# One tile for state and u, the centring of v in a matmul, and the substitution's blocks stored straight from the masked scores

## The chip, the cores and the metric

The kernel runs on one core of one Trainium2 chip. TensorE (PE), VectorE (DVE), ScalarE (ACT) and GpSimd (POOL) compute; SyncE (SP) issues every DMA of this kernel, in order, and 16 DMA engines move the data. The metric is the time of one execution on the device in microseconds (us), the median of three runs.

## The reference

The program is a decoder trunk of two layers on a sequence of 1024 positions with 1024 channels, in float32. Layer 1 is an RWKV-7 mixer: projections r, k, v and a gate g of token-shifted inputs, two small low-rank paths for decay and a, and then a recurrence per head (16 heads of 64), cut to what matters here:

```python
kk = kk / max(sqrt(sum(kk * kk)), 1e-12)            # per head
state = state * w_t + sa * b_t + v_t * k_t           # sa = state . a_t, a = -kk, b = kk * ah
y_t = state . r_t
yn = (y - mean(y)) * rsqrt(var(y) + eps)             # per head, so v may be centred beforehand
```

The normalized y, a bonus and silu(g) go through an output matrix. Layer 2 is differential attention on keys and values from layer 1's output. Both layers end in a residual sum.

## The kernel before

Layer 1 begins with norms, low-rank paths and the first projections (about 0 to 260 us). Then the recurrence runs in chunks of 64 positions. A tile is 2 chunks of 8 heads (4 pairs); 16 tiles go one after another, software-pipelined over slots: in slot i, `chain` works on tile i, `norm` on tile i-1, `merge` on tile i+1, `invert` on tile i+2 and `prep` on tile i+3. Between their instructions stand those of the remaining projections and of the output projection (`proj_step`, `out_proj`), which give PE most of its work. Layer 2 follows from about 900 us on.

The order on each engine is not written out by hand: every instruction is recorded, and a planner that simulates the engines, with priorities for chain, merge, invert and prep, sets the order in which each engine, SP too, meets its instructions. Engines then work strictly in that order.

The parts that the change touches:

- `proj_step`, projection of v (p == 2): the 128x512 result `ev` is transposed in four pieces on PE (L211), DVE sums each head's 64 values (L215), subtracts the mean while it copies to SBUF (L217), and SP stores the centred v to DRAM, `d_vc` (L220). Tiles `ev` come from a pool `evp` with two buffers, which the output projection also uses (loads of x, stores of x2).
- `prep`: the masked scores `pm` hold, for each chunk, the triangular blocks (32 by 32) that a forward substitution has to invert. The squared norms of k come from a matmul with the matrix `last`, which puts them in row 31 of each block and zeros elsewhere; ACT copies them into `ab` (L485), DVE adds the masked scores (L510), and one DMA stores `ab` to DRAM as `dA` (L511). L528 reads `dA` back as `al`, 4 copies for 4 groups of partitions.
- `invert`: DVE divides by the norms (L538 to L540), POOL substitutes row by row (L551, L553), SP stores `xx` as `dX` (L556) and loads it in another layout as `qd` (L558), which `merge` needs (L576 on DVE).
- `merge` and `chain`: `uv` holds v and, later, u; `sv` holds v again (copied by ACT, L608) and the state. The chain is z (L639), a copy (L642), u (L649), copies into `uv` (L651, L652), the state's update (L658, L661, L665, L666), and the output y from two groups of matmuls (L629 from the state, L632 from u and v).

```python
        nc.sync.dma_start(out=dA.rearrange("c x s t -> (x s) c t"), in_=ab)          # L511
        nc.sync.dma_start(out=dX.rearrange("x k q t -> q x k t"), in_=xx)            # L556
        nc.sync.dma_start(out=al, in_=dA.rearrange("c x s t -> (c x) (s t)").unsqueeze(0).to_broadcast([4, 32, 1024])) # L528
```

SP meets a DMA, waits for the semaphores that it needs, and issues it; whatever stands behind it waits too.

Of the kernel before, what the change touches and what calls it, by code (L numbers as in the profile page):

```python
# [20 lines left out]
P = 128  # L21
# [3 lines left out]
C = 64  # L25
# [51 lines left out]
class Trunk:  # L77
# [10 lines left out]
    def start(self, lp, xnT):  # L88

        nc, tc, I = self.nc, self.tc, self.I  # L90
        const = self.const
        self.ident = const.tile([P, P], F32, name="ident")
        make_identity(nc, self.ident)
        self.par = const.tile([P, len(ROWS), KT], F32, name="par")
# [14 lines left out]
        for t0 in range(0, KT, 2):  # L109
            ms = lp.tile([P, 2], F32, name="ms")  # L110
            for i in range(2):
                sq = lp.tile([P, D], F32, name="sq", bufs=1)
# [3 lines left out]
            for i in range(2):  # L116
# [5 lines left out]
                for hf in range(2):  # L122
                    pt = self.fps.tile([P, 4, P], F32, name="fl")
# [36 lines left out]
    def proj_step(self, hf, p, pr, src, group):  # L160

        nc, I = self.nc, self.I
        sl = slice(hf * TH, (hf + 1) * TH)
        G = {"w": []}
# [31 lines left out]
        def post(k):  # L196
            if k == 0:
                G["ev"] = ev = self.evp.tile([P, TH], F32, name="ev")
                if p == 3:
                    nc.scalar.activation(ev, G["ps"], AF.Sigmoid)  # L200
                    nc.vector.tensor_tensor(ev, ev, G["ps"], op=ALU.mult)
                else:
                    nc.scalar.copy(out=ev, in_=G["ps"])
                nc.sync.dma_start(out=self.d_in[p][pr, :, sl], in_=ev)
            if p != 2:
                return

            if k == 2:
                G["pt"] = pt = self.fps.tile([P, 4, P], F32, name="fl")
                for i in range(4):  # L210
                    nc.tensor.transpose(out=pt[:, i, :], in_=G["ev"][:, i * P:(i + 1) * P], identity=self.ident)  # L211
            if k == 4:
                ptv = G["pt"].rearrange("p i (h e) -> p (i h) e", e=64)
                mn = self.evp.tile([P, 8], F32, name="mn")
                nc.vector.tensor_reduce(mn, ptv, axis=AX.X, op=ALU.add)  # L215
                vc = self.evp.tile([P, 4, P], F32, name="ev")
                nc.vector.scalar_tensor_tensor(vc.rearrange("p i (h e) -> p (i h) e", e=64),  # L217
                                               mn.unsqueeze(2).to_broadcast([P, 8, 64]), -1.0 / 64, ptv,
                                               op0=ALU.mult, op1=ALU.add)
                nc.sync.dma_start(out=self.d_vc[sl, pr * P:(pr + 1) * P].rearrange("(i p) e -> p i e", p=P), in_=vc)  # L220
# [174 lines left out]
    def wkv_open(self):  # L395
        nc, tc = self.nc, self.tc
# [26 lines left out]

        self.last = cst.tile([P, P], F32, name="last")
        nc.gpsimd.memset(self.last, 0.0)
        for o in (0, 64):
            nc.gpsimd.memset(self.last[o:o + 64, o + 31:o + 64:32], 1.0)
# [15 lines left out]
    def prep(self, M, following):  # L443
# [31 lines left out]
        nc.tensor.matmul(nps.rearrange("p c t -> p (c t)"), lhsT=self.last, rhs=sq.rearrange("p u t -> p (u t)"), start=True, stop=True)  # L475
# [56 lines left out]
    def invert(self, M):  # L532
# [24 lines left out]
        M["qd"] = qd = self.ub.tile([P, 8, 32], F32, name="qd", bufs=1)  # L557
        nc.sync.dma_start(out=qd, in_=dX.rearrange("(c x) k q t -> (x k q) c t", c=8))  # L558

    def merge(self, M):  # L560
# [6 lines left out]
        M["sv"] = sv = self.ub.tile([P, 2, 8, C], F32, name="sv")  # L567
# [39 lines left out]
        for h in range(2):  # L607
            nc.scalar.copy(out=sv[64 - h * 64:P - h * 64, h], in_=uv[64 - h * 64:P - h * 64, h])  # L608

    def chain(self, M):  # L610

        nc, sm, ps = self.nc, self.sm, self.wps
        ar, pm, uv, sv, bkt, q, wc = (M[n] for n in ("ar", "pm", "uv", "sv", "bkt", "q", "wc"))
        HS = [slice(h * 64, h * 64 + 64) for h in range(2)]
        wt = self.state[M["j"]]
        for h in range(2):
            nc.scalar.copy(out=sv[HS[h], h, 0::NC, :], in_=wt[HS[h]])
        yield 1

        def out(c):  # L620
            if c == 0:
                M["y"] = ps.tile([P, 8, C], F32, name="y", bufs=1)
            y = M["y"]

            z = M["qt"] + c == 0
            pairs = [(u * NC + c, h) for u in range(NU) for h in range(2)]

            for uc, h in [] if z else pairs:
                nc.tensor.matmul(y[HS[h], uc, :], lhsT=sv[HS[h], h, uc, :], rhs=ar[HS[h], uc, 1, :], start=uc == c, stop=False,  # L629
                                 tile_position=(h * 64, h * 64))  # L630
            for uc, h in pairs:
                nc.tensor.matmul(y[HS[h], uc, :], lhsT=uv[:, h, uc, :], rhs=pm[:, h, uc, 64:P], start=z and uc == c,  # L632
                                 stop=uc == pairs[-1][0], tile_position=(0, h * 64))
        for c in range(NC):
            us = [(u, u * NC + c) for u in range(NU)]
            zp = ps.tile([P, NU, C], F32, name="zu", bufs=2)
            for u, uc in us:
                for h in range(2):
                    nc.tensor.matmul(zp[HS[h], u, :], lhsT=pm[:, h, uc, 0:64], rhs=sv[:, h, uc, :], start=True, stop=True,  # L639
                                     tile_position=(0, h * 64))  # L640
            zs = sm.tile([P, NU, C], F32, name="zs", bufs=1)
            nc.scalar.copy(out=zs, in_=zp)  # L642
            if c:
                out(c - 1)
# [9 lines left out]
            if M["qt"] < S // TM - 1 or c < NC - 1:  # L654
                sp = ps.tile([P, NU, C], F32, name="zu", bufs=2)
                for u, uc in us:
                    for h in range(2):
                        nc.tensor.matmul(sp[HS[h], u, :], lhsT=bkt[:, h, uc, :], rhs=uv[:, h, uc, :], start=True, stop=True,  # L658
                                         tile_position=(0, h * 64))
                tn = sm.tile([P, NU, C], F32, name="tn", bufs=1)  # L660
                nc.vector.tensor_tensor(tn, wt, sp, op=ALU.add)  # L661
                wb = wc[:, c::NC].unsqueeze(2).to_broadcast([P, NU, C])
                if c < NC - 1:
                    for h in range(2):
                        nc.vector.tensor_tensor(sv[HS[h], h, c + 1::NC, :], tn[HS[h]], wb[HS[h]], op=ALU.mult)  # L665
                nc.gpsimd.tensor_tensor(wt, tn, wb, op=ALU.mult)  # L666
            yield 1
        out(NC - 1)

    def norm(self, M):  # L670
# [3 lines left out]
        y = nm.tile([P, NU, TM], F32, name="yt")  # L674
        nc.scalar.copy(out=y.rearrange("p u (c t) -> p (u c) t", t=C), in_=M["y"])
# [54 lines left out]
    def layer1(self):  # L730
# [12 lines left out]
        self.evp = st.enter_context(tc.tile_pool(name="evp", bufs=2, side="right", reuse_waits="tile"))  # L743
# [38 lines left out]
        for i in range(-3, 17):  # L782
# [555 lines left out]
```

## Time and profile before

| | |
|---|---|
| median of 3 runs | 1633.85 us (1627.41 to 1634.28) |
| the profiled execution | 1635.44 us, its span 1633.6 us |
| busy share of the span | PE 91%, DVE 73%, ACT 56%, POOL 41% |
| PE busy, 1100 to 1200 us (layer 2) | 99.63 of 100 us |
| PE busy, 800 to 900 us (last tiles) | 82.39 of 100 us |
| mean granted TensorE clock | 0.945 of full speed |

Busy time is that of instructions; a PE that is busy is not a PE at its peak. L12 is line 12 of the kernel before. The clock is granted at full (2.4 GHz) or half (1.2 GHz); a stretch's number is a mean of the two. An idle time stands in brackets, with what ended it.

### The profile page before, as it was taken

The numbers are of one execution on the slowest core, as the hardware profiler recorded it, in microseconds if no ns is written. First come the engines' busy times: TensorE is split into PE (matmuls) and PEld (weight loads), VectorE is DVE, ScalarE is ACT, GpSimd is POOL, SyncE is SP. The second block draws the span as 40 slices with busy tenths as digits, with TensorE's granted clock in tenths as the row PEclk, the third lists the DMA queues.
The fourth block names the chain that finished last, engine by engine and source line by source line (L and its number), as shares of the span: only waits on it lengthen the run. The fifth ranks groups of instructions, "written<-read, shape, count | busy, mean of one in ns | idle before, by whom it ended". The sixth has DMA issues, their size and how long they took to land.

```text
span 1633.6 us, 31095 instructions
## 1 busy us (share of the span) xinstructions
PE 1494.4 (91%) x10496; PEld 1208.3 (74%) x10496; DVE 1194.8 (73%) x3119; ACT 909.6 (56%) x2095; POOL 672.8 (41%) x1685
## 2 busy tenths in 40 slices
PE   3799999988998999979869789999999999999897
PEld 3577777666776777768758567788888888888786
DVE  7745658866879798788555777887878888787764
ACT  5645565745657586655234644665565656556420
POOL 4000003856878688778656111233232333333100
PEclk8799999989999999979879789999999999999999
DMA  7654677755656567656446451211111111113231
GB/s 195 187 185 144 186 226 216 201 163 152 194 157 175 164 179 190 185 160 174 128 142 164 131 169 58 67 46 31 46 46 27 46 33 40 40 40 119 92 126 52
DMA packets 218095, 207.39 MB, mean 127 GB/s; under 512 B 78032, under 2 KB 163280, under 8 KB 217936
## 3 DMA queue, kind: packets, MB, share of 16 engines
q1 hardware_dynamic: 217936, 205.40, 42.9%
q8 instruction: 83, 1.36, 0.3%
q14 instruction: 76, 0.62, 0.1%
HBM read 147.09 MB, written 58.27 MB: 126 GB/s over the span
## 4 chain that ended last, share of the span: by engine, by line
PE 63%; DVE 14%; DMA 7%; ACT 6%; issue 5%; POOL 4%; SPq 1%; ACTq 0%; DVEq 0%; POOLq 0%
PE pj L878 6%; PE pj L877 6%; PE pj L879 6%; PE fl L192 5%; PE fl L193 5%; PE fl L194 5%; PE tr L982 4%; PE sc L940 2%; PE sc L941 2%; PE tr L970 2%; POOL xx L553 2%; POOL tm L551 2%; DMA al<-dA 1%; PE sc L498 1%; PE tr L1255 1%
## 5 line engine op out<-in xcount | busy, mean ns | idle before, releaser
L192 PE MATMUL fl<-xh,wh 128*128 128x512 f32 x512 | 212.2, 420 | 11.2 <-DVE ev L217 8.8
L877 PE MATMUL pj<-wh,xh 128*128 128x512 f32 x512 | 214.1, 418 | 0.0
L193 PE MATMUL fl<-xl,wh 128*128 128x512 f32 x512 | 209.2, 410 | 3.7 <-DVE xl L151 3.7
L553 POOL TENSOR_TENSOR xx<-xx,tm 128x60 f32<-128x60 f32 (+24 forms) x496 | 196.8, 397 | 36.4 <-DVE xx L545 0.4
L194 PE MATMUL fl<-xh,wl 128*128 128x512 f32 x512 | 209.3, 410 | 0.0
L551 POOL TENSOR_TENSOR tm<-al,xx 128x60 f32<-128x60 f32 (+24 forms) x496 | 190.2, 383 | 40.4 <-DVE xx L545 4.0
L878 PE MATMUL pj<-wh,xl 128*128 128x512 f32 x512 | 202.7, 396 | 2.6 <-DVE xl L1216 2.6
L879 PE MATMUL pj<-wl,xh 128*128 128x512 f32 x512 | 202.1, 396 | 0.0
L157 DVE TENSOR_TENSOR wl<-wf,wh 128x512 fp32r<-128x512 f32 x160 | 119.0, 748 | 80.4 <-ACT wh L156 79.5
L946 ACT ACTIVATE p<-sc,mx 128x256 f32<-128x256 f32 (+7 forms) x128 | 94.6, 741 | 142.1 <-DVE mx L945 123.1
L926 POOL CAST kh<-kh 64x128 fp32r<-64x128 f32 x128 | 45.2, 353 | 263.4 <-ACT kh L918 250.0
L156 ACT CAST wh<-wf 128x512 fp32r<-128x512 f32 x160 | 97.6, 617 | 94.1 <-PE fl L193 71.6
L192 PEld LDWEIGHTS fl<-xh,wh 128*128 128x128 f32 x512 | 98.4, 192 | 40.3 <-issue 12.4
L193 PEld LDWEIGHTS fl<-xl,wh 128*128 128x128 f32 x512 | 99.0, 193 | 29.2 <-DVE xl L151 5.2
L194 PEld LDWEIGHTS fl<-xh,wl 128*128 128x128 f32 x512 | 98.7, 193 | 24.0 <-issue 1.4
L879 PEld LDWEIGHTS pj<-wl,xh 128*128 128x128 f32 x512 | 96.8, 189 | 21.9
L878 PEld LDWEIGHTS pj<-wh,xl 128*128 128x128 f32 x512 | 97.5, 190 | 19.6 <-DVE xl L1216 4.3
L877 PEld LDWEIGHTS pj<-wh,xh 128*128 128x128 f32 x512 | 97.5, 190 | 15.4 <-ACT xh L1215 0.2
L944 DVE TENSOR_REDUCE mx<-sc 128x1 f32<-128x256 f32 (+7 forms) x128 | 95.4, 753 | 0.8
L982 PEld LDWEIGHTS tr<-v,p 128*128 128x128 f32 x576 | 74.9, 194 | 7.8 <-ACT p L972 3.2
L982 PE MATMUL tr<-v,p 128*128 128x128 f32 x576 | 76.1, 278 | 2.1 <-ACT p L972 2.1
L940 PE MATMUL sc<-kh,q 128*128 128x512 f32 (+2 forms) x192 | 70.9, 378 | 4.0 <-issue 2.1
(295 smaller groups left out, 3695.3 us busy)
## 6 DMA issues: line engine op xcount, KB each, us to landing
wf<-in_a_w_in SPq DMA_DIRECT2D x64, 512.0 KB
d_in<-ev SPq DMA_DIRECT2D x64, 256.0 KB
wf<-in_b_w SPq DMA_DIRECT2D x64, 256.0 KB
xk<-d_xn SPq DMA_DIRECT2D x40, 256.5 KB
al<-dA SPq DMA_DIRECT2D x16, 512.0 KB
wf<-in_a_w_out SPq DMA_DIRECT2D x16, 512.0 KB
p<-d_x SPq DMA_DIRECT2D x10, 512.0 KB
d_c<-cc SPq DMA_DIRECT2D x16, 260.0 KB
```

Source lines behind the costliest of these rows:

```text
L156: self.nc.scalar.copy(out=wh, in_=wf)
L157: self.nc.vector.tensor_tensor(wl, wf, wh.bitcast(F32), op=ALU.subtract)
L192: nc.tensor.matmul(G["ps"], lhsT=wh[:, kk, :], rhs=xh, start=(k == 0), stop=False)
L193: nc.tensor.matmul(G["ps"], lhsT=wh[:, kk, :], rhs=xl, start=False, stop=False)
L194: nc.tensor.matmul(G["ps"], lhsT=wl[:, kk, :], rhs=xh, start=False, stop=(k == KT - 1))
L551: nc.gpsimd.tensor_tensor(tv, al[:, s:s + 1, s + 1:].to_broadcast([P, n, w]), xx[:, 0:n, s:s + 1].to_broadcast([P, n, w]), op=ALU.mult)
L553: nc.gpsimd.tensor_tensor(xx[:, 0:n, s + 1:], xx[:, 0:n, s + 1:], tv, op=ALU.add)
L877: nc.tensor.matmul(pf, lhsT=self.X[i][0][:, k], rhs=wh, start=(k == 0), stop=False)
L878: nc.tensor.matmul(pf, lhsT=self.X[i][1][:, k], rhs=wh, start=False, stop=False)
L879: nc.tensor.matmul(pf, lhsT=self.X[i][0][:, k], rhs=wl, start=False, stop=(k == KT - 1))
L940: nc.tensor.matmul(sc[:, b:e], lhsT=q[:, m], rhs=H["kh"][:, m, b:e], start=True, stop=False)
L982: nc.tensor.matmul(po, lhsT=at[:, b, :], rhs=H["v"][:, b, :], start=(b == 0), stop=(b == i))
```

## The change

Five things change. (1) v is transposed and centred in one step: the transposes become matmuls with `less`, the identity minus 1/64 in each head's block; DVE only copies the result out. (2) `sv` is gone: the state lies in the half of `uv` that u overwrites later, and the y matmuls that read the state stand ahead of u's copies; those that read u stand behind the state's update, in the same chunk. (3) `ab` and the adds are gone: four DMAs store the blocks' first 31 rows directly from `pm`, 31 partitions each, and two more store the norms (row 31), which a matmul with `bones` puts into every partition, from partitions 0 and 64. (4) `evp` has three buffers for two, `qd` two for one. (5) The copy of y to SBUF moves from `norm` into `chain`, and the planner's step counts of `chain` and `merge` are one lower.

```diff
+        nc.gpsimd.tensor_tensor(self.less, self.less, self.ident, op=ALU.add)
...
-                    nc.tensor.transpose(out=pt[:, i, :], in_=G["ev"][:, i * P:(i + 1) * P], identity=self.ident)
+                    nc.tensor.matmul(pt[:, i, :], lhsT=G["ev"][:, i * P:(i + 1) * P], rhs=self.less, start=True, stop=True)
...
-                nc.vector.tensor_reduce(mn, ptv, axis=AX.X, op=ALU.add)
                 vc = self.evp.tile([P, 4, P], F32, name="ev")
-                nc.vector.scalar_tensor_tensor(vc.rearrange("p i (h e) -> p (i h) e", e=64),
-                                               mn.unsqueeze(2).to_broadcast([P, 8, 64]), -1.0 / 64, ptv,
-                                               op0=ALU.mult, op1=ALU.add)
+                nc.vector.tensor_copy(out=vc, in_=G["pt"])
...
-        nc.tensor.matmul(nps.rearrange("p c t -> p (c t)"), lhsT=self.last, rhs=sq.rearrange("p u t -> p (u t)"), start=True, stop=True)
+        nc.tensor.matmul(nps.rearrange("p c t -> p (c t)"), lhsT=self.bones, rhs=sq.rearrange("p u t -> p (u t)"), start=True, stop=True)
...
-        ab = tp.tile([P, 8, 32], F32, name="ab")
-        for b in range(4):
-            nc.scalar.copy(out=ab[32 * b:32 * b + 32], in_=nps[32 * b:32 * b + 32, :, b % 2 * 32:b % 2 * 32 + 32])
+        ab = tp.tile([P, 8, 2, 32], F32, name="ab")
+        nc.scalar.copy(out=ab[0:65].rearrange("p c b t -> p c (b t)"), in_=nps[0:65])
+        for h in range(2):
+            nc.sync.dma_start(out=dA[:, 2 * h:2 * h + 2, 31, :].unsqueeze(0), in_=ab[64 * h:64 * h + 1])
...
         for b in range(4):
-            bs = slice(32 * b, 32 * b + 32)
-            nc.vector.tensor_tensor(ab[bs], ab[bs], pm[bs, b // 2, :, b % 2 * 32:b % 2 * 32 + 32], op=ALU.add)
-        nc.sync.dma_start(out=dA.rearrange("c x s t -> (x s) c t"), in_=ab)
+            bs = slice(32 * b, 32 * b + 31)
+            nc.sync.dma_start(out=dA[:, b, 0:31, :].rearrange("c s t -> s c t"), in_=pm[bs, b // 2, :, b % 2 * 32:b % 2 * 32 + 32])
...
-        M["qd"] = qd = self.ub.tile([P, 8, 32], F32, name="qd", bufs=1)
+        M["qd"] = qd = self.ub.tile([P, 8, 32], F32, name="qd", bufs=2)
...
-        for h in range(2):
-            nc.scalar.copy(out=sv[64 - h * 64:P - h * 64, h], in_=uv[64 - h * 64:P - h * 64, h])
...
+            for uc, h in [] if z else pairs:
+                nc.tensor.matmul(y[HS[h], uc, :], lhsT=uv[HS[h], h, uc, :], rhs=ar[HS[h], uc, 1, :], start=uc == c, stop=False,
+                                 tile_position=(h * 64, h * 64))
...
-        self.evp = st.enter_context(tc.tile_pool(name="evp", bufs=2, side="right", reuse_waits="tile"))
+        self.evp = st.enter_context(tc.tile_pool(name="evp", bufs=3, side="right", reuse_waits="tile"))
```

The planner makes a new order from it. On SP, around the blocks of one tile in the middle of the recurrence, this stood before (a name ends in the tile's shape as the DMA's destination walks it, slowest first):

```order
L556 DMA dX<-xx 4x256x32
L168 DMA wf<-in_a_w_in 128x1024
L748 DMA xk<-d_xn_70 128x513 x2
L558 DMA qd<-dX 128x8x32
L748 DMA xk<-d_xn_70 128x513
L511 DMA dA<-ab 128x8x32
L168 DMA wf<-in_a_w_in 128x1024
L204 DMA d_in_63<-ev 128x512
L441 DMA a<-d_a 128x4x128
L528 DMA al<-dA 128x1x1024
```

And this stands there now, around the blocks of a tile a little later:

```order
L547 DMA dX<-xx 4x256x32
L683 DMA d_o<-yt 128x4x128
L662 DMA bv<-d_bv 128x512
L502 DMA dA<-pm 31x8x32 x4
L549 DMA qd<-dX 128x8x32
L169 DMA wf<-in_a_w_in 128x1024
L205 DMA d_in_63<-ev 128x512
L519 DMA al<-dA 128x1x1024
```

One store of 128 partitions has become four of 31; the load of `qd` and that of the next weights stand behind them, and `al`, which waits for all of `dA`, three places further on.

On PE, one chunk of a chain among the output projection's matmuls (L285 to L287) stood like this before, z and the state's part of y first and u (L649) behind:

```order
L639 MATMUL zu<-sv,pm 64x64
L629 MATMUL y<-ar,sv 64x64
L639 MATMUL zu<-sv,pm 64x64 x7
L629 MATMUL y<-ar,sv 64x64 x7
L285 MATMUL fl<-wh,xh 128x256 x2
L286 MATMUL fl<-wh,xl 128x256
L287 MATMUL fl<-wl,xh 128x256
L285 MATMUL fl<-wh,xh 128x256
L286 MATMUL fl<-wh,xl 128x256
L287 MATMUL fl<-wl,xh 128x256
L285 MATMUL fl<-wh,xh 128x256
L649 MATMUL zu<-zs,q 64x64 x8
```

Now one chunk's end and the next one's beginning stand like this:

```order
L629 MATMUL zu<-zs,q 64x64 x8
L666 MATMUL mg<-bones,y_10267 128x2 x4
L638 MATMUL zu<-uv,bkt 64x64
L648 MATMUL y<-pm,uv 64x64
L638 MATMUL zu<-uv,bkt 64x64 x7
L648 MATMUL y<-pm,uv 64x64 x7
L617 MATMUL zu<-uv,pm 64x64
L623 MATMUL y<-ar,uv 64x64
L617 MATMUL zu<-uv,pm 64x64 x7
L623 MATMUL y<-ar,uv 64x64 x7
```

The state's part of y (L629 before, L623 now) already stood directly with z; it has not moved against u.

## Rows read from the trace of the kernel before

**Rows 1.** Busy time of each engine, the 16 tiles: us, count; clock, DMA share, GB/s

```profile
260.00:880.00 620.00, 558.91 (x5560) 444.29 (x5560) 461.68 (x1037) 358.31 (x732) 451.48 (x1077) 0.92 0.61 172
...
820.00:840.00 20.00, 11.08 (x137) 9.42 (x135) 10.17 (x29) 4.46 (x10) 8.19 (x21) 0.66 0.57 164
```

**Rows 2.** PE in order of time: start, us, instruction, idle time before it and releaser

```profile
368.10 0.76 PE L192 MATMUL fl<-xh,wh 128*128 128x512 f32 x1 [5.10 <-DVE ev L217]
...
402.88 0.47 PE L192 MATMUL fl<-xh,wh 128*128 128x512 f32 x1 [1.94 <-DVE ev L217]
...
792.62 0.58 PE L285 MATMUL fl<-wh,xh 128*128 128x256 f32 x1 [7.09 <-DVE ev L291]
...
831.68 0.44 PE L639 MATMUL zu<-sv,pm 128*64 128x64 f32 x2 [8.92 <-DVE sv L665]
```

**Rows 3.** DVE in order of time, at two of these places

```profile
402.05 0.69 DVE L217 SCALAR_TENSOR_TENSOR ev<-mn,fl 128x512 f32<-128x512 f32 x1 [5.83 <-DMA d_vc<-ev]
...
830.70 0.43 DVE L259 TENSOR_TENSOR xm<-xm,xk 128x256 f32<-128x256 f32 x1 [8.22 <-DMA xm<-d_o]
```

**Rows 4.** SP's queue in order of time: start, us that the issue took, DMA

```profile
325.22 4.87 SPq L441 DMA_DIRECT2D kk<-d_in  x1
...
351.73 7.63 SPq L220 DMA_DIRECT2D d_vc<-ev  x1
...
388.98 0.55 SPq L528 DMA_DIRECT2D al<-dA  x1
389.62 0.55 SPq L556 DMA_DIRECT2D dX<-xx  x1
390.36 8.91 SPq L220 DMA_DIRECT2D d_vc<-ev  x1
399.32 0.50 SPq L441 DMA_DIRECT2D v<-d_in  x1
...
776.75 9.74 SPq L239 DMA_DIRECT2D wf<-in_a_w_out  x1
...
817.97 9.11 SPq L526 DMA_DIRECT2D d_bv<-v  x1
```

**Rows 5.** Busy time by stretch, as rows 1: two us while `al` moves

```profile
391.00:393.00 2.00, 2.00 (x35) 1.35 (x34) 1.96 (x8) 1.94 (x6) 1.30 (x4) 1.00 0.25 82
```

**Rows 6.** SP's queue, one tile's stores of `dX` and `dA` and their readers

```profile
471.36 0.56 SPq L556 DMA_DIRECT2D dX<-xx  x1
...
476.30 0.37 SPq L558 DMA_DIRECT2D qd<-dX  x1
478.29 0.37 SPq L511 DMA_DIRECT2D dA<-ab  x1
480.51 0.56 SPq L528 DMA_DIRECT2D al<-dA  x1
```

**Rows 7.** Groups by line: shapes, count; busy us, mean ns; idle before, releasers

```profile
L510 DVE TENSOR_TENSOR ab<-ab,pm 32x256 f32<-32x256 f32 x64 | 26.9, 421 | 0.9
...
L485 ACT COPY ab<-sc 32x256 f32<-32x256 f32 x64 | 23.2, 362 | 3.9 <-PE sc L475 3.2
...
L608 ACT COPY sv<-uv 64x512 f32<-64x512 f32 x32 | 19.7, 616 | 11.5 <-DMA uv<-d_vc 11.1
...
L215 DVE TENSOR_REDUCE mn<-fl 128x8 f32<-128x512 f32 x16 | 11.0, 689 | 11.0 <-PE fl L211 10.9
...
L217 DVE SCALAR_TENSOR_TENSOR ev<-mn,fl 128x512 f32<-128x512 f32 x16 | 10.9, 681 | 6.0 <-DMA d_vc<-ev 5.8
...
L974 DVE COPY p<-tr 128x512 f32<-128x512 f32 x8 | 5.5, 685 | 0.2 <-PE tr L970 0.2
```

**Rows 8.** Groups by line on PE

```profile
L982 PE MATMUL tr<-v,p 128*128 128x128 f32 x576 | 76.1, 278 | 2.1 <-ACT p L972 2.1
...
L629 PE MATMUL y<-ar,sv 64*64 64x64 f32 x480 | 25.7, 232 | 0.4 <-ACT yt L675 0.2
...
L211 PE MATMUL fl<-ident,ev 128*128 128x128 f32 x64 | 11.3, 298 | 0.5 <-ACT ev L203 0.5
```

**Rows 9.** Who waited for whom: us in total, times, longest

```profile
DVE ni L538 <- DMA al<-dA: 11.9, 5, 5.2
```

More of the change, by code (lines that the diff above doesn't have):

```diff
@@ L422, in wkv_open @@
         nc.gpsimd.memset(self.bones[64:P, 64:P], 1.0)
[L424 to L427, printed above, removed]
         self.omka = cst.tile([P, KT], F32, name="omka")
@@ L566, in merge @@
         M["uv"] = uv = self.ub.tile([P, 2, 8, C], F32, name="uv")
-        M["sv"] = sv = self.ub.tile([P, 2, 8, C], F32, name="sv")
         e0 = NU * M["j"] * P
@@ L606, in merge @@
             yield 0
-        for h in range(2):
-            nc.scalar.copy(out=sv[64 - h * 64:P - h * 64, h], in_=uv[64 - h * 64:P - h * 64, h])
     def chain(self, M):
         nc, sm, ps = self.nc, self.sm, self.wps
-        ar, pm, uv, sv, bkt, q, wc = (M[n] for n in ("ar", "pm", "uv", "sv", "bkt", "q", "wc"))
+        ar, pm, uv, bkt, q, wc = (M[n] for n in ("ar", "pm", "uv", "bkt", "q", "wc"))
         HS = [slice(h * 64, h * 64 + 64) for h in range(2)]
@@ L616, in chain @@
         for h in range(2):
-            nc.scalar.copy(out=sv[HS[h], h, 0::NC, :], in_=wt[HS[h]])
+            nc.scalar.copy(out=uv[HS[h], h, 0::NC, :], in_=wt[HS[h]])
         yield 1
[L620 to L633, printed above, removed]
+        M["y"] = y = ps.tile([P, 8, C], F32, name="y", bufs=1)
         for c in range(NC):
             us = [(u, u * NC + c) for u in range(NU)]
+            pairs = [(uc, h) for _, uc in us for h in range(2)]
+            z = M["qt"] + c == 0
             zp = ps.tile([P, NU, C], F32, name="zu", bufs=2)
@@ L638, in chain @@
                 for h in range(2):
-                    nc.tensor.matmul(zp[HS[h], u, :], lhsT=pm[:, h, uc, 0:64], rhs=sv[:, h, uc, :], start=True, stop=True,
+                    nc.tensor.matmul(zp[HS[h], u, :], lhsT=pm[:, h, uc, 0:64], rhs=uv[:, h, uc, :], start=True, stop=True,
                                      tile_position=(0, h * 64))
@@ L642, in chain @@
             nc.scalar.copy(out=zs, in_=zp)
-            if c:
-                out(c - 1)
+            for uc, h in [] if z else pairs:
+                nc.tensor.matmul(y[HS[h], uc, :], lhsT=uv[HS[h], h, uc, :], rhs=ar[HS[h], uc, 1, :], start=uc == c, stop=False,
+                                 tile_position=(h * 64, h * 64))
             yield 1
@@ L664, in chain @@
                     for h in range(2):
-                        nc.vector.tensor_tensor(sv[HS[h], h, c + 1::NC, :], tn[HS[h]], wb[HS[h]], op=ALU.mult)
+                        nc.vector.tensor_tensor(uv[HS[h], h, c + 1::NC, :], tn[HS[h]], wb[HS[h]], op=ALU.mult)
                 nc.gpsimd.tensor_tensor(wt, tn, wb, op=ALU.mult)
+            for uc, h in pairs:
+                nc.tensor.matmul(y[HS[h], uc, :], lhsT=uv[:, h, uc, :], rhs=pm[:, h, uc, 64:P], start=z and uc == c,
+                                 stop=uc == pairs[-1][0], tile_position=(0, h * 64))
             yield 1
-        out(NC - 1)
+        M["yt"] = self.nm.tile([P, NU, TM], F32, name="yt")
+        nc.scalar.copy(out=M["yt"].rearrange("p u (c t) -> p (u c) t", t=C), in_=y)
     def norm(self, M):
@@ L673, in norm @@
         j, t0 = M["j"], M["qt"] * TM
-        y = nm.tile([P, NU, TM], F32, name="yt")
-        nc.scalar.copy(out=y.rearrange("p u (c t) -> p (u c) t", t=C), in_=M["y"])
+        y = M["yt"]
         y2 = nm.tile([P, NU, TM], F32, name="y2", bufs=1)
@@ L742, in layer1 @@
         self.xmp = st.enter_context(tc.tile_pool(name="xmp", bufs=XB, side="right", reuse_waits="tile"))
-        self.evp = st.enter_context(tc.tile_pool(name="evp", bufs=2, side="right", reuse_waits="tile"))
+        self.evp = st.enter_context(tc.tile_pool(name="evp", bufs=3, side="right", reuse_waits="tile"))
+        self.less = self.evp.tile([P, P], F32, name="less", bufs=1)
+        nc.gpsimd.memset(self.less, 0.0)
+        for o in (0, 64):
+            nc.gpsimd.memset(self.less[o:o + 64, o:o + 64], -1.0 / 64)
         def src_of(hf):
@@ L786, in layer1 @@
             if 0 <= i < 16:
-                st_.append((self.chain(Ms[i]), 8, 0, T))
+                st_.append((self.chain(Ms[i]), 7, 0, T))
             if 0 <= i - 1 < 16:
@@ L790, in layer1 @@
             if 0 <= i + 1 < 16:
-                st_.append((self.merge(Ms[i + 1]), 9, 2, T))
+                st_.append((self.merge(Ms[i + 1]), 8, 2, T))
             if 0 <= i + 3 < 16:
```

2 lines of the change are left out of this document (removed).

## The prediction

> **What bounds the kernel now.** I read the busy time by stretch first, then PE in order of time for its gaps, and from each gap back to DVE and to SP's queue. Layer 2 keeps PE busy and is not touched. The 16 tiles are where time can move: of 620 us there PE is busy 558.91, at a mean granted clock of 0.92, DVE 461.68, POOL 451.48, ACT 358.31, and the DMA engines 0.61 of the time [rows 1]. So PE has the most work and still idles 61 us. The four stretches where it idles longest at one go or in a cluster (5.10, 1.94, 7.09 and 8.92 us, 23.05 in all, [rows 2]) all end 3.6 to 8.7 us after the end of the same thing on SP's queue, an issue that took 7.63, 8.91, 9.74 and 9.11 us, where 0.5 is usual [rows 4]. The row at 390 shows why: `al` and then `dX` had just been issued, and the next DMA was not accepted until they were nearly through. The late loads and stores then hold DVE (5.83 us for the buffer that `d_vc` still reads, 8.22 us for `xm`, [rows 3]), and DVE holds PE. After the last of them the clock falls too: 0.66 in the 20 us from 820 on, with 11.08 us of PE work in them [rows 1]. A blocked issue of 4.87 us, at 325, has no such gap behind it [rows 2, 4].
>
> So two kinds of DMA are dear although they are small, `al` and `dX`, and the reason is in the rows: while `al` moves alone the DMA share is 0.25, four engines of sixteen [rows 5]. Its source has 4 as the slowest dimension (four copies of `dA`), and `dX`'s destination has it too (4x256x32 in the order). A transfer whose slowest dimension is 128 has no such limit.
>
> **The change part by part.** The sum is made against the profiled execution's 1635.4 us, which stands 1.6 above the median.
>
> *The blocks' stores.* Before, `dA` had 128 as slowest dimension, 1024 runs of 32 floats. `al` waits for it and was issued 2.22 us behind it; `qd`, which waits for `dX` with its 1024 runs of the same size, 4.94 us behind `dX` [rows 6]. With sixteen engines a run count of 64 each and with four 256 each, the difference is 2.72 us for 192 runs, 14.2 ns a run. Now there are four stores of 31x8x32, 992 runs. No row shows 31 as slowest dimension. The lower bound is sixteen engines as for `dA`, 2.2 us; `dX`'s four engines would give 4.9; the upper bound is one engine, 2.22 + (992 - 64) x 14.2 ns = 15.4 us. I take one engine: both counts seen, 4 of 4 and 16 of 128, divide the slowest dimension, so that every engine has the same share, and 31 has no divisor up to 16 but 1.
>
> The Trainium skill (DMA: Bandwidth & Descriptors, section "Why a DMA increments its semaphore by 16 and not by 1") states this rule: a hardware-issued DMA runs on the largest number of engines up to 16 that divides the slowest dimension of both sides, with 127 partitions as an example that gets one. For `al` the rule gives 4, and the share of 0.25 agrees; by it the stores get one engine and the sum below stands, and by the other reading, that 31 rows spread like 128, the term below would be nothing. No run here has shown 31 yet.
>
> How long is SP blocked? In the case at 390, `al` (512 KB at 82 GB/s, [rows 5], 6.4 us) and `dX` (256 x 14.2 ns = 3.6 us) make 10.0 us, and SP was free for the next DMA 10.3 us after it issued `al` (399.32 less 388.98, [rows 4]). So SP is held for about as long as the narrow transfers take. Four stores on one engine take 992 x 14.2 ns = 14.1 us, less the three issues that are SP's own time and what the queue can hold: I take 11 us per tile (0 to 14). In the new order the loads of `qd` and of weights stand right behind the four stores, and `al` waits for their landing.
>
> What does PE lose? The four blocks of before add up to 35.4 us, and the gaps behind them to 23.05: 0.65 us per us. The third buffer of `evp` takes away the way by which two of them reached PE (L217), which leaves 16.0 us, 0.45 per us. An 11 us block costs between 5.0 and 7.2 us; I take 6. The first three tiles' stores come before any chain runs and beside projections with weights in store, so I count 13 tiles: 13 x 6 = +78 us (0 to 16 x 11 = 176).
>
> *The norms' stores.* Two more DMAs of one partition each and three more of blocks cost SP some 0.4 us each [rows 6], 2 us per tile of a queue that otherwise waits for others: 0 in the sum, up to 2 per tile.
>
> *v's centring.* 64 transposes at 11.3 / 64 = 0.18 us become float32 matmuls; L982 has such, 288 in 576 rows, 76.1 us, 0.26 each [rows 8]. +5.6 us of PE, of which I count 5, since PE has few gaps where they stand (0 to 6). On DVE 16 sums and 16 subtractions (11.0 + 10.9 us) become 16 copies of 0.685 us, 11.0 [rows 7]. The PE gaps behind L217 (5.10 and 1.94) go with the third buffer: -6 (0 to -7).
>
> *Work that goes.* DVE loses L510's 26.9 and the 10.9 above, 37.8 us; ACT loses L485's 23.2 and L608's 19.7, and gains 16 copies of 65 partitions, by L608's 616 ns 9.9: 33.0 us [rows 7]. Neither is the bound: DVE is busy 74% of the stretch, ACT 58% [rows 1]. DVE's saving is 8% of its work there, and 8% of PE's 61 idle us is 5; I take twice that for both engines, -10 (0 to -38, all of DVE's).
>
> *State and u in one tile.* u's copies must now wait for the state's y matmuls, 25.7 us in 30 groups, 0.86 us each [rows 8]. The order had these already ahead of u, so nothing (0 to +26). The copy of y and the matmul with `bones` only change place or matrix; `qd`'s second buffer and `less` are left out of the sum.
>
> Sum: 1635.4 + 78 + 5 - 6 - 10 = 1702, and 1.6 less for a median: 1701 us.
>
> **The rivals.**
>
> *The stores are hidden, and the change is not slower.* If they run on sixteen engines, or if SP's loads lie far enough ahead (a block of 4.87 us cost PE nothing), the term of 78 goes: 1635 + 5 - 6 - 10 = 1624, and 1596 if all of DVE's 38 us counted. It decides where a block is shorter than about 5 us, that is from three or more engines on. For it: all of the work on DVE and ACT that goes; against it: 31 in the order, the four gaps behind the four blocks.
>
> *The stores cost what the rest gives back.* With the block half covered, 13 x 1 to 2 us: 1635 + 5 - 16 + 13 = 1637.
>
> *The substitution becomes the bound.* `al` comes 13.2 us later (15.4 less 2.2), and DVE, which stands in order, already waited for it five times of 16 [rows 9]; POOL has 451 us of work in 620, so 10 us per tile to spare. If that is used up by the waits for `qd`, each of 13 tiles is longer by the whole 13: 1635 + 169 + 5 - 16 = 1793. Against it: substitution and chain are a slot apart, so lateness is partly taken up once and not per tile.
>
> **How the numbers follow.** The forecast has 0.60 (its own range 1655 to 1775), the substitution as bound 0.13, the hidden stores 0.19, the balance 0.08. The range of 8 in 10 reaches down to 1620, through most of the hidden case, and up to 1790. Within 0.5% (8 us, about what a measurement of this kernel can tell) lie the balance and a little of the others: 0.08. Faster 0.19, slower 0.73.
>
> **What would show it.** Right: SP's issues behind the four stores take about 8 us or more in most tiles; the DMA share there is near 0.06 when nothing else moves; PE's gaps in the tiles' stretch grow from 61 us to well over 100 at a lower mean clock, while layer 2 takes what it took; DVE has some 38 us less work, ACT 33, and PE's instructions for v's transposes take about 17 us for 11. Wrong: `al` is issued about 2 to 5 us behind the last store as before, with no long issue between; then the first rival holds. If DVE's wait for `al` becomes its longest, and POOL's idle time ends with it, the third holds.

## The result, and the profile after

The changed kernel takes 1763.08 us (median of 4 runs, 1761.21 to 1767.44) against 1632.68 of the kernel before in the same session: a ratio of 1.0809, 95% interval [1.0775, 1.0842]. It is slower, as forecast, by 130 us where 67 were forecast; the time lies inside the range of 1620 to 1790. The profiled execution took 1761.6 us.

The page of the changed kernel, whole span: busy time of each engine with its share and count, then the granted clock in 40 slices:

```profile
span 1759.7 us, 31138 instructions
...
PE 1535.2 (87%) x10560; PEld 1241.0 (71%) x10560; DVE 1156.1 (66%) x3039; ACT 874.7 (50%) x2015; POOL 652.9 (37%) x1686
...
PEclk7899999779898798887898878999999999999999
```

The page of the kernel before, span 1633.6 us, has:

```profile
PE 1494.4 (91%) x10496; PEld 1208.3 (74%) x10496; DVE 1194.8 (73%) x3119; ACT 909.6 (56%) x2095; POOL 672.8 (41%) x1685
```

DVE's work fell by 38.7 us, ACT's by 34.9. PE has more, 1535.2 for 1494.4, and it idles 224.5 us (span less busy) for 139.2. So the 126 us that the span grew by are 85 us of idle PE and 41 us of more PE work. Where, the busy times by stretch of the changed kernel show (columns as in [rows 1]):

```profile
260.00:880.00 620.00, 490.52 (x4347) 378.60 (x4345) 361.75 (x791) 282.35 (x569) 354.14 (x857) 0.85 0.53 142
...
520.00:522.00 2.00, 2.00 (x12) 1.08 (x14) 1.85 (x7) 1.15 (x3) 1.77 (x5) 1.00 0.10 11
...
1200.00:1300.00 100.00, 99.62 (x542) 83.49 (x541) 81.67 (x256) 60.06 (x173) 32.15 (x95) 1.00 0.14 43
```

In the 620 us of [rows 1] PE now idles 129.5 us instead of 61, at a mean clock of 0.85 instead of 0.92. Layer 2 is as full as it was. SP's queue shows what happens once per tile; this is a tile in the middle (start, us that the issue took, DMA; x4 is four issues in a row):

```profile
513.48 0.37 SPq L549 DMA_DIRECT2D qd<-dX  x1
513.94 8.67 SPq L502 DMA_DIRECT2D dA<-pm  x4
522.67 2.82 SPq L205 DMA_DIRECT2D d_in<-ev  x1
525.59 0.38 SPq L169 DMA_DIRECT2D wf<-in_a_w_in  x1
527.43 0.57 SPq L519 DMA_DIRECT2D al<-dA  x1
```

The four stores and the issue behind them hold SP for 11.6 us, and `al` is issued 13.5 us after the first store, where [rows 6] have 2.2 from `dA` to `al`. Both are short cases: over the 16 tiles the median is 15.9 us (13.0 to 26.2), and before it was 4.9 (2.2 to 16.1). The 2 us from 520 on, above, lie inside: DMA moves 11 GB/s, which is one store's 31 KB in 2.8 us, the time that each issue now waits. From the first issue of `al` to the last the 16 tiles take 675.9 us instead of 555.5: 120 of the 130 us are here, 8.0 per tile.

Two ways lead from the held queue to PE. The first is `al`: DVE, which works in order, waits for it. DVE of the changed kernel, in order of time, with the idle time and what ended it in brackets:

```profile
538.77 0.18 DVE L529 TENSOR_SCALAR ni<-al 128x32 f32<-128x32 f32 x1 [13.13 <-DMA al<-dA]
...
819.80 0.69 DVE L255 TENSOR_TENSOR xm<-xm,xk 128x512 f32<-128x512 f32 x1 [16.74 <-DMA xm<-d_o]
```

The second row is the other way: a load for the output projection that needs nothing from the stores but stands behind them. SP's queue ahead of it:

```profile
792.59 10.94 SPq L502 DMA_DIRECT2D dA<-pm  x4
803.62 2.79 SPq L235 DMA_DIRECT2D wf<-in_a_w_out  x1
...
808.42 0.57 SPq L519 DMA_DIRECT2D al<-dA  x1
809.05 0.98 SPq L252 DMA_DIRECT2D xm<-d_o  x2
```

And PE of the changed kernel, in order of time, four of its longest gaps:

```profile
539.60 0.79 PE L194 MATMUL fl<-xl,wh 128*128 128x512 f32 x1 [7.31 <-DVE xl L152]
...
592.37 0.58 PE L490 MATMUL sc<-ar,bk 64*128 64x128 f32 x1 [14.84 <-ACT ab L475]
...
726.24 0.80 PE L193 MATMUL fl<-xh,wh 128*128 128x512 f32 x1 [13.25 <-DVE ev L202]
...
821.20 0.58 PE L281 MATMUL fl<-wh,xh 128*128 128x256 f32 x1 [14.83 <-ACT xh L249]
```

The gap that ends at 539.60 follows DVE's wait for `al` (L152 stands right behind L529 on DVE). Those at 821.20 and 726.24 follow waits for `xm` (16.74 us, above, and 12.47 us), that at 592.37 a wait of 17.07 us of ACT for `cc`, a load issued at 580.13, again behind the stores. Once it is issued, `al` comes no later than before: DVE's waits for it end 8.6 to 11.7 us after its issue, and 10.7 to 12.0 before (waits of over 1 us). But `xm` at 809.05 and `cc` at 580.13 stand right behind `al` too (808.42 and 578.93), and DVE and ACT had them 10.7 and 10.9 us after their issue, where the waits for `xm` of before ended after 2.2 to 6.0; so part of these two waits seems to be `al`'s own transfer. In the list of waits, `al` grew from [rows 9] to:

```profile
DVE ni L529 <- DMA al<-dA: 67.2, 8, 16.9
```

### The profile page after: what moved, and what is told of

The parts are those of the page before. It is cut to its first block, busy times and chain, and to the rows that moved or that the text cites. A ratio compares the mean times of both kernels' runs of the same rounds, so it can differ in the third digit from the quotient of the medians.

```text
span 1759.7 us, 31138 instructions
## 1 busy us (share of the span) xinstructions
PE 1535.2 (87%) x10560; PEld 1241.0 (71%) x10560; DVE 1156.1 (66%) x3039; ACT 874.7 (50%) x2015; POOL 652.9 (37%) x1686
## 4 chain that ended last, share of the span: by engine, by line
PE 36%; DVE 5%; DMA 5%; ACT 3%; issue 3%; POOL 3%; SPq 1%; ACTq 0%; POOLq 0%; DVEq 0%
PE pj L865 5%; PE pj L866 5%; PE pj L867 5%; PE tr L970 3%; PE sc L928 2%; PE tr L958 2%; PE sc L929 2%; DMA dX<-xx 2%; POOL xx L544 1%; PE tr L1243 1%; PE tr L1244 1%; PE tr L1242 1%; POOL tm L542 1%; PE pj L1244 1%; PE pj L1243 1%
## 5 line engine op out<-in xcount | busy, mean ns | idle before, releaser
L193 PE MATMUL fl<-xh,wh 128*128 128x512 f32 x512 | 217.8, 431 | 24.7 <-DVE ev L202 15.1
L194 PE MATMUL fl<-xl,wh 128*128 128x512 f32 x512 | 218.6, 427 | 8.5 <-DVE xl L152 8.5
L195 PE MATMUL fl<-xh,wl 128*128 128x512 f32 x512 | 214.6, 420 | 0.0
L542 POOL TENSOR_TENSOR tm<-al,xx 128x60 f32<-128x60 f32 (+24 forms) x496 | 182.0, 367 | 44.0 <-DVE xx L536 8.3
L544 POOL TENSOR_TENSOR xx<-xx,tm 128x60 f32<-128x60 f32 (+24 forms) x496 | 182.2, 367 | 37.0 <-DVE xx L536 0.4
L158 DVE TENSOR_TENSOR wl<-wf,wh 128x512 fp32r<-128x512 f32 x160 | 114.9, 722 | 109.4 <-ACT wh L157 107.9
L193 PEld LDWEIGHTS fl<-xh,wh 128*128 128x128 f32 x512 | 102.2, 200 | 53.3 <-DVE ev L202 15.7
L194 PEld LDWEIGHTS fl<-xl,wh 128*128 128x128 f32 x512 | 102.4, 200 | 37.8 <-DVE xl L152 10.9
L866 PEld LDWEIGHTS pj<-wh,xl 128*128 128x128 f32 x512 | 97.6, 191 | 18.8 <-DVE xl L1204 3.3
L490 PE MATMUL sc<-ar,bk 64*128 64x128 f32 x512 | 64.3, 324 | 35.5 <-DVE pm L494 15.8
L490 PEld LDWEIGHTS sc<-ar,bk 64*128 64x128 f32 x512 | 53.9, 220 | 50.2 <-DVE pm L494 17.4
L281 PE MATMUL fl<-wh,xh 128*128 128x256 f32 x192 | 60.0, 320 | 24.6 <-ACT xh L249 14.8
```

The costliest lines, as they stand in the source:

```text
L158: self.nc.vector.tensor_tensor(wl, wf, wh.bitcast(F32), op=ALU.subtract)
L193: nc.tensor.matmul(G["ps"], lhsT=wh[:, kk, :], rhs=xh, start=(k == 0), stop=False)
L194: nc.tensor.matmul(G["ps"], lhsT=wh[:, kk, :], rhs=xl, start=False, stop=False)
L195: nc.tensor.matmul(G["ps"], lhsT=wl[:, kk, :], rhs=xh, start=False, stop=(k == KT - 1))
L490: nc.tensor.matmul(pp[h][:, i, :], lhsT=bkh(h, c), rhs=ar[h * 64:h * 64 + 64, c].rearrange("p z t -> p (z t)"), start=True, stop=True)
L542: nc.gpsimd.tensor_tensor(tv, al[:, s:s + 1, s + 1:].to_broadcast([P, n, w]), xx[:, 0:n, s:s + 1].to_broadcast([P, n, w]), op=ALU.mult)
```

## The experiments

Theory: the four stores of 31 partitions run on one DMA engine each, hold SP's queue, and this alone makes the loss. Rivals: the count of DMAs or of their runs; `al`'s lateness, and not the queue; another part of the change. Each ratio stands against the kernel before, run on the same chip in between. In the edits, `...` stands for text left out.

The table gathers what the verdicts rest on. "SP's issues" adds up the time of every single DMA issue on SP over the whole execution, from the trace's records (a row of SP's queue that stands for several issues also holds the pauses between them, so its second column can't be added up). "PE idle" is span less busy time.

| kernel | median us | ratio [95%] | SP's issues | PE idle | DVE's wait for `al` |
|---|---|---|---|---|---|
| before | 1632.7 | 1 | 379.3 | 139.2 | 11.9 |
| changed | 1763.1 | 1.0809 [1.0775, 1.0842] | 585.5 | 224.5 | 67.2 |
| changed, stores of 32 | 1651.2 | 1.0111 [1.0068, 1.0154] | 436.7 | 135.3 | 16.7 |
| changed, stores of 16 + 15 | 1654.8 | 1.0106 [1.0076, 1.0136] | 452.5 | 144.1 | 24.0 |
| before, `dA` in 31 + 1 | 1770.5 | 1.0833 [1.0787, 1.0879] | 592.0 | 240.5 | 35.1 |
| before + unread stores of 31 | 1764.4 | 1.0796 [1.0754, 1.0838] | 593.2 | 217.9 | 55.8 |
| before + unread stores of 32 | 1640.1 | 1.0049 [1.0027, 1.0071] | 427.3 | 134.2 | 13.3 |
| before + unread stores of 31, later | 1738.3 | 1.0658 [1.0614, 1.0702] | 603.4 | 207.1 | 6.5 |

**The changed kernel with stores of 32 partitions.** Row 31 goes along with the block and the norms get a DRAM tile and a load of their own.

```diff
-            bs = slice(32 * b, 32 * b + 31)
-            nc.sync.dma_start(out=dA[:, b, 0:31, :].rearrange(...), in_=pm[bs, ...])
+            bs = slice(32 * b, 32 * b + 32)
+            nc.sync.dma_start(out=dA[:, b, :, :].rearrange(...), in_=pm[bs, ...])
```

> The changed kernel, but the four block stores have 32 partitions for 31 (row 31 goes along unused), and the norms go to a small DRAM tile of their own, loaded beside al; everything else of the change stays. Theory (31 partitions put a store on one DMA engine, SP is held behind it): no issue above 4 us directly behind the stores, DVE's wait for al back near 12 us, and the time falls by 100 us or more from 1763, to 1600 to 1650. Rival 1 (many more issues on SP, or the small runs themselves): it stays above 1720, since it issues one DMA more per tile. Rival 2 (the shared tile of state and u, the planner's step counts or the new order make the chain late): it stays above 1700.

1651.19 us, 1 us above the range expected: one partition more per store takes 112 us off. What is left of the change costs 18. The page:

```profile
span 1644.9 us, 31105 instructions
...
PE 1509.6 (92%) x10560; PEld 1220.2 (74%) x10560; DVE 1160.3 (71%) x3039; ACT 880.8 (54%) x2019; POOL 675.6 (41%) x1686
```

**The kernel before, its store cut into 31 and 1.** The rest of the change is absent.

```diff
-        nc.sync.dma_start(out=dA.rearrange("c x s t -> (x s) c t"), in_=ab)
+        for b in range(4):
+            nc.sync.dma_start(out=dA[:, b, 0:31, :].rearrange("c s t -> s c t"), in_=ab[32 * b:32 * b + 31])
+            nc.sync.dma_start(out=dA[:, b, 31, :].unsqueeze(0), in_=ab[32 * b + 31:32 * b + 32])
```

> The kernel before with one thing changed: ab goes to dA in four stores of 31 partitions and four of one partition (row 31), for one store of 128. No work is saved anywhere. Theory (one engine per store, SP held 9 to 11 us per tile, and al late): 1720 to 1800, so that the stores alone account for the loss. Rival 1 (issues): seven more issues of 0.4 us per tile, 45 us of SP in all, mostly hidden, under 1660. Rival 2 (the rest of the change is what costs): 1625 to 1650.

1770.53 us: the narrow stores alone make the whole loss.

**The changed kernel with the old store.** `ab`, its copies and adds and the single store are back, all else stays changed.

```diff
         for b in range(4):
-            bs = slice(32 * b, 32 * b + 31)
-            nc.sync.dma_start(out=dA[:, b, 0:31, :].rearrange("c s t -> s c t"), in_=pm[bs, ...])
+            bs = slice(32 * b, 32 * b + 32)
+            nc.vector.tensor_tensor(ab[bs], ab[bs], pm[bs, ...], op=ALU.add)
+        nc.sync.dma_start(out=dA.rearrange("c x s t -> (x s) c t"), in_=ab)
```

> The changed kernel with the old way of the blocks (four copies on ACT, four additions on DVE, one store of 128 partitions); v's centring in the matmul, the shared tile, three ev buffers and the step counts stay. Theory: the loss is gone, and what DVE and ACT save (11 us and 20 us) and the third ev buffer are worth 5 to 30 us: 1600 to 1635. Rival 2 (shared tile, steps, order): above 1700.

1646.55 us, 1.0077 [1.005, 1.0104]: without the new stores the change is near the kernel before, but above it, and above the 1600 to 1635 expected.

**The kernel before with four unread stores of 31, and of 32, partitions** to a scratch tile beside `dA`'s store.

```diff
+        dZ = self.dr.tile([8, 4, 32, 32], F32, name="dZ")
+        for b in range(4):
+            bs = slice(32 * b, 32 * b + 31)          # 32 in the second kernel
+            nc.sync.dma_start(out=dZ[:, b, 0:31, :].rearrange("c s t -> s c t"), in_=pm[bs, ...])
```

> The kernel before, and behind its store of dA four more stores of 31 partitions by 8 by 32 floats from the masked scores to a DRAM tile that nothing reads. al waits for the old store alone, so nothing in the data waits for the new ones. It tells SP's and the engine's being held from al's waiting for the landing. If the held queue is most of the loss: 1700 to 1780. If the late landing of dA (al, and with it the substitution) is most of it: under 1670. al stands behind them in the queue all the same, so it is later by the part of the 11 us that it cannot jump.

> The same as the run with four idle stores (that nothing reads) behind dA, but with 32 partitions each for 31: 1024 runs for 992 and as many issues. If it is the one engine that costs, and neither the number of issues nor of runs: within 1% of before, 1625 to 1650, against 1764 with 31. If the extra issues or runs cost: above 1700.

1764.40 and 1640.14 us. Same issues, 32 runs of 1024 fewer, and 124 us more. The same tile in both, on SP's queue; first with 31:

```profile
521.09 6.50 SPq L515 DMA_DIRECT2D dZ<-pm  x3
527.69 2.77 SPq L562 DMA_DIRECT2D qd<-dX  x1
530.51 0.72 SPq L515 DMA_DIRECT2D dZ<-pm  x1
531.33 2.45 SPq L511 DMA_DIRECT2D dA<-ab  x1
...
536.50 0.56 SPq L532 DMA_DIRECT2D al<-dA  x1
```

and with 32:

```profile
476.47 3.02 SPq L515 DMA_DIRECT2D dZ<-pm  x3
480.54 0.38 SPq L562 DMA_DIRECT2D qd<-dX  x1
480.98 0.57 SPq L515 DMA_DIRECT2D dZ<-pm  x1
481.64 0.40 SPq L511 DMA_DIRECT2D dA<-ab  x1
...
483.87 0.55 SPq L532 DMA_DIRECT2D al<-dA  x1
```

Nobody reads `dZ`, and yet everything behind it is late: `al` is issued 15.4 us after the first of these stores for 7.4. So the count of DMAs or runs (8 us) is not the cause, and nothing has to wait for the stores' data. But `al` is late here too, so this pair doesn't part the queue from `al`. The next run does.

**The same unread stores, but of `qd` and behind its load**, so that `al` is seldom among the DMAs that they hold.

```diff
         nc.sync.dma_start(out=qd, in_=dX.rearrange("(c x) k q t -> (x k q) c t", c=8))
+        dZ = self.dr.tile([8, 4, 32, 32], F32, name="dZ")
+        for b in range(4):
+            bs = slice(32 * b, 32 * b + 31)
+            nc.sync.dma_start(out=dZ[:, b, 0:31, :].rearrange("c s t -> s c t"), in_=qd[bs])
```

> The kernel before with four more stores per tile of 31x8x32 to a scratch place, as in the run with unread stores from the masked scores, but of qd and behind its load: 20 to 30 places behind the tile's dA and al in SP's order, so that al is not held behind them in the same slot. Theory A (it is the held queue that costs, wherever in the tile it is held: weights, stores and loads of the projections behind it come late): 1740 to 1775 us, with DVE's wait for al staying near the 12 us of before and SP's issue time up by 110 to 150 us. Theory B (the loss comes by way of al: the substitution starts late and DVE, which stands in order, waits): 1640 to 1690 us at the same SP issue time. Between the two, say 1700 to 1730, the loss has both parts.

1738.27 us, just under what theory A expects and far above theory B. SP is held, by 224 us of issues more than in the kernel before, which is above the 110 to 150 expected; this is one tile of it:

```profile
462.60 9.16 SPq L562 DMA_DIRECT2D dZ<-qd  x4
471.80 2.83 SPq L204 DMA_DIRECT2D d_in<-ev  x1
474.73 0.38 SPq L168 DMA_DIRECT2D wf<-in_a_w_in  x1
```

while DVE's wait for `al` is below that of before:

```profile
DVE ni L538 <- DMA al<-dA: 6.5, 5, 2.4
```

So the held queue costs most of the loss without `al`, but not at the same price. Against the kernel with stores of 32 it has 176.1 us more of SP's issues and takes 98 us more: 0.56 us per us. (That kernel is a control in the number of stores, not in their place; 32 partitions at this place were not tried.) Where the hold delays `al` as well, a us costs more: 124.3 us for 165.9 with the unread stores, 111.9 for 148.8 with the change's own, 0.75 both times. That `al` makes this difference is argued, not shown: at the two places other DMAs stand behind the stores too, and the kernel with `dA` in 31 + 1 loses as much with a wait for `al` of only 35.1 us.

**The changed kernel, each store split into 16 and 15 partitions.** Twice the issues, the same runs.

```diff
-            bs = slice(32 * b, 32 * b + 31)
-            nc.sync.dma_start(out=dA[:, b, 0:31, :].rearrange(...), in_=pm[bs, ...])
+            for s0, s1 in ((0, 16), (16, 31)):
+                bs = slice(32 * b + s0, 32 * b + s1)
+                nc.sync.dma_start(out=dA[:, b, s0:s1, :].rearrange(...), in_=pm[bs, ...])
```

> The changed kernel, where each store of 31 partitions is split into one of 16 and one of 15: the same runs of 32 floats, twice the issues (eight per tile), nothing else. Theory A (what counts is how many engines a store gets, a divisor of its slowest dimension: 31 gives 1, 16 and 15 give 16 and 15): the loss of about 115 to 138 us goes and 1640 to 1660 us is left, with no issue over 3 us behind these stores. Rival (a store of fewer partitions than 32, or of a count that is no power of two, is slow as such, or the count of DMAs is what costs): 1760 us or more. If only the 15 is slow (one engine), about 1700 us.

1654.75 us, as with 32 partitions. Eight stores are through SP in half the time that four took, and `al` follows 6.1 us after the first:

```profile
528.26 4.51 SPq L503 DMA_DIRECT2D dA<-pm  x8
532.87 0.35 SPq L169 DMA_DIRECT2D wf<-in_a_w_in  x1
533.32 0.85 SPq L737 DMA_DIRECT2D xk<-d_xn  x2
534.35 0.57 SPq L520 DMA_DIRECT2D al<-dA  x1
```

It is not that fewer than 32 partitions are slow: 31 is. That is what the Trainium skill says (DMA: Bandwidth & Descriptors, section "Why a DMA increments its semaphore by 16 and not by 1"): as many engines, up to 16, as divide the slowest dimension. 16, 15 and 32 then get 16, 15 and 16 engines, 31 gets one, and the runs agree. The records of single packets show it too: in the 2 us of the changed kernel from 520 on, where the stores run alone, never more than 2 packets are under way, while the stores of 16 + 15 have up to 22 at once (529.5 to 530 us) and those of 32 up to 25 (524 to 525 us).

**What is left of the change: shared tile, third buffer, centring.** All three kernels have the old store of the blocks. The first has the shared tile for state and u, the step counts and `qd`'s buffer alone; the second adds the third `evp` buffer; with the centring in the matmul it would be the run with the old store above. Against that run:

```diff
-                    nc.tensor.matmul(pt[:, i, :], lhsT=G["ev"][:, i * P:(i + 1) * P], rhs=self.less, start=True, stop=True)
+                    nc.tensor.transpose(out=pt[:, i, :], in_=G["ev"][:, i * P:(i + 1) * P], identity=self.ident)
...
-                nc.vector.tensor_copy(out=vc, in_=G["pt"])
+                nc.vector.tensor_reduce(mn, ptv, axis=AX.X, op=ALU.add)
+                nc.vector.scalar_tensor_tensor(vc..., mn..., -1.0 / 64, ptv, op0=ALU.mult, op1=ALU.add)
...
-        self.evp = st.enter_context(tc.tile_pool(name="evp", bufs=3, side="right", reuse_waits="tile"))
+        self.evp = st.enter_context(tc.tile_pool(name="evp", bufs=2, side="right", reuse_waits="tile"))   # 3 in the second
```

> The kernel before with the shared tile of state and u, the chain's new order and step counts and qd's second buffer alone: v's centring, the two ev buffers and the blocks' store are those of before. With the old store the changed kernel stood at 1646.6, 14 us above before, though it had less work. If the shared tile or the new order is what costs there: 1640 to 1655. If the centring in the matmul (more PE work) costs it: 1615 to 1635.

> The changed kernel with the old store of the blocks and the old centring, but the third evp buffer: it differs from the shared-tile run (1634.8 us) by that buffer alone, and from the old-store run (1646.6 us) by the centring alone. My forecast of the term on the third buffer was -6: then 1629 us. If the third buffer costs (it lets projections' and stores' DMAs start earlier and collide), 1640 to 1650 us and the centring matmul is free. If it does nothing, 1633 to 1637 us, and the matmul form of the centring costs about 12 us.

1634.76 us, 1.0015 [0.9994, 1.0036], and 1636.12 us beside 1637.22, 0.9992 [0.9973, 1.0011]. The shared tile costs nothing. The third buffer's gain of 0.2% is within the intervals; the 1629 us forecast for it did not come. The centring takes 0.9992 to 1.0077, 14 us; these two kernels differ in nothing else. The first fence is the page of the kernel without it, the second with it:

```profile
span 1630.7 us, 31024 instructions
...
PE 1497.1 (92%) x10496; PEld 1209.2 (74%) x10496; DVE 1195.2 (73%) x3119; ACT 897.8 (55%) x2067; POOL 671.5 (41%) x1685
```

```profile
span 1644.7 us, 31133 instructions
...
PE 1505.5 (92%) x10560; PEld 1223.6 (74%) x10560; DVE 1187.9 (72%) x3103; ACT 893.5 (54%) x2065; POOL 671.3 (41%) x1689
```

PE has 8.4 us more work and 5.6 more idle time, DVE 7.3 us less work; what makes the idle time was not pursued.

**Wide `al` and `dX`.** Before and after, these two run on four engines ([rows 5]: a share of 0.25). Here `al` is loaded by four DMAs of 32 partitions and `dX` stored by four; once in the kernel before, once in the changed kernel with stores of 32, once in that with the old centring and two buffers.

```diff
-        nc.sync.dma_start(out=al, in_=dA.rearrange("c x s t -> (c x) (s t)").unsqueeze(0).to_broadcast([4, 32, 1024]))
+        for g in range(4):
+            nc.sync.dma_start(out=al[32 * g:32 * g + 32], in_=dA.rearrange("c x s t -> (c x) s t"))
...
-        nc.sync.dma_start(out=dX.rearrange("x k q t -> q x k t"), in_=xx)
+        for g in range(4):
+            nc.sync.dma_start(out=dX[:, :, g, :], in_=xx[32 * g:32 * g + 32])
```

> The kernel before with al in four loads of 32 partitions and dX in four stores of 32, nothing else. Theory: SP's issues above 7 us are gone, PE's four gaps with them: 1590 to 1620. Rival (six more issues per tile cost what the width gains): 1625 to 1650.

> The changed kernel with the 32-row stores and the norms' own tile, and now also the two narrow transfers that before has: al comes in four loads of 32 partitions for one with a slowest dimension of 4, dX goes in four stores of 32 partitions. Six more issues per tile, some 3 us of SP. Theory: the four blocks of 7.6 to 9.7 us that before has go too, with the 23 us of PE's gaps and the falls of the clock behind them: 1590 to 1630, under before. Rival: SP's issues have become the limit, or al's and dX's width is hidden: 1640 to 1660 as with the 32-row stores alone.

> The version with 32-partition stores and wide al and dX, which ran at 1599.3 us, with v's centring put back to transposes, DVE sums and subtractions, and two evp buffers. Theory A (the matmul form of the centring and what it does to the order cost about 12 us, the gap between the run with the old store and the run with the shared tile alone): 1585 to 1595 us, the fastest of all. Theory B (the 12 us lie elsewhere, in the order of the day, and DVE's saved 22 us count): 1600 to 1612 us. If 1597 to 1602, the centring is neutral in this surrounding.

1606.78 us, 0.9843 [0.9827, 0.986]; 1599.28 us, 0.9794 [0.977, 0.9817]; 1603.12 us, 0.9787 [0.9762, 0.9812]. Spread over more engines, two DMAs that the change doesn't touch give 26 us: the kernel before has 16 single issues of over 2 us (66.5 us in all), the first of these three has none, and its PE idles 110.8 us for 139.2. The last two beat both kernels and can't be told apart, so in this surrounding the centring and the third buffer together show no cost: the 14 us do not belong to the centring everywhere. The pages of the first and the second:

```profile
span 1603.7 us, 31261 instructions
...
PE 1492.9 (93%) x10496; PEld 1205.1 (75%) x10496; DVE 1200.1 (75%) x3119; ACT 910.3 (57%) x2095; POOL 681.8 (43%) x1685
```

```profile
span 1602.9 us, 31318 instructions
...
PE 1494.1 (93%) x10560; PEld 1209.5 (75%) x10560; DVE 1162.3 (73%) x3039; ACT 878.0 (55%) x2017; POOL 669.1 (42%) x1686
```

## Why the prediction was right, and where its size failed

*Direction and mechanism: right, and shown.* One engine for 31, SP held, late loads and stores, PE starved. Four stores to `al`'s issue were forecast at 15.4 us at most; the median of the 16 tiles is 15.9. That the stores would be hidden (0.19) is refuted.

*The step that failed: "I take 6" us of PE per tile for an 11 us block, +78 us.* The stores cost 112 us (the changed kernel with 31 against 32) to 138 (the kernel before with the narrow stores alone). The hold was sized well: 13 x 11 = 143 us forecast, 148.8 us more of SP's issues measured between 31 and 32. That is 9.3 in each of 16 tiles, so two errors, in the tiles counted and in the hold of one, happened to cancel. Its price was too low: 6 us for 11, 0.55 us per us (0.45 to 0.65), forecast, 0.75 measured. The price came from the four blocks of [rows 4], and two things are missing in it.

First, and with the larger part, it counted idle PE alone. Between 31 and 32 partitions PE's idle time differs by 89.2 us (224.5 and 135.3) and its busy time by 25.6 (1535.2 and 1509.6) for the same number of PE instructions, at a mean granted clock of 0.913 and 0.941. So 0.60 of a us per us is idle time, which the forecast has, and 0.17 is slower work at the lower clock. The prediction saw the clock fall behind a gap ([rows 1], 0.66) and gave it no term: its 78 us stand against 89 of idle PE and 26 of slower work.

Second, in the case at 390 `al` and `dX` themselves made the block and had been issued: that hold did not delay `al`. Where the added hold leaves `al` alone, 0.56 was measured, by number the price forecast, though slower work is in it too (PE's idle time 72.9 us, its busy time 15.1 us more); where `al` is behind the stores, 0.75. The lateness of `al` stood in the prediction as a rival with a chance of 0.13, as if it were either that or the queue. It seems to be both, added up: about three quarters by the queue and one by `al`, if the whole difference between the two places is put down to `al`, which no run shows.

*"Work that goes", -10, and the third buffer, -6.* DVE's and ACT's work fell by 38.7 and 34.9 us (37.8 and 33.0 forecast), and no gain can be told: the changed kernel with stores of 32, in which it fell by 34.5 and 28.8 (1160.3 and 880.8 us busy), idles PE 135.3 us for 139.2, 4 less, where its own runs lie up to 7 us apart (1646.67 to 1653.80). The shared tile alone takes 16.5 us off ACT (893.1) and nothing off the time (1.0015). The buffer's worth is not told from zero. That the gaps behind L217 are gone means only that others stand in their place.

*v's centring, +5.* The matmuls take PE 18.8 us for 11.3 (16.9 forecast); with what follows it costs 14 us in one surrounding and, together with the third buffer, nothing in another. *State and u in one tile, 0:* right, 1.0015.

So the sum went wrong as follows: 78 became 112, and +5 - 6 - 10 became +18, the rest of the change in the kernel with stores of 32; 130 in all.

*What was to show it.* SP's long issues: yes, in all 16 tiles. PE's idle time in the tiles' stretch: 129.5, "well over 100". DVE -38, ACT -33: yes. The DMA share: 0.10 and not 0.06, at the rate of one store in 2.8 us. The share counts packets and not engines: one or two were under way, 1.59 on average, and 1.59 of 16 is 0.10. DVE's wait for `al` rose to 67.2 us, its longest for any DMA but not its longest wait (107.9 us, for ACT's `wh`), so the mark set for the third rival was met in part, as the experiments have it.

## What to carry to other kernels

Before a store is cut, look at its slowest dimension: 31 rows cost 112 us more than 32, and 16 + 15 rows cost no more than 32. A small DMA that runs on few engines costs what stands behind it on its queue, whether or not anyone reads it; price a hold with the late loads that it causes and the clock that falls with the gaps, and take the price from a case in which the same things stand behind it. Work taken from engines that are not the bound (here 63 us) gave back nothing that could be told from zero; widening two DMAs of before, which took no work away, gave 26.

## What was not expected of the hardware

An issue on SP's queue is held for 2.8 us behind each narrow store (2.82, 2.79, 2.77 and 2.83 in the rows above): SP gets no further ahead of these stores than one or two of them. 31 KB in 992 / 4 = 248 runs make 11.3 ns a run, not far from the 14.2 of the prediction. And the hold passes on to a DMA of 128 partitions that has nothing to do with the stores and runs on many engines (before, up to 26 of its packets were under way at once): `dA`'s own store took 2.45 us to issue for 0.40. The Trainium skill (DMA: Bandwidth & Descriptors, section "Why a DMA increments its semaphore by 16 and not by 1") says that a DMA on few engines takes the lowest-numbered ones; then all these stores, and a part of each wide DMA, meet on one engine. No run here tells the engines apart.
